# Softmax scaling of an attention kernel moved from ScalarE to GpSimd

## The chip, the cores and the metric

The kernel runs on one NeuronCore of a Trainium2 chip. Five engines work side by side, each through its own queue in order: TensorE (PE: matrix products and transposes, results in PSUM), VectorE (DVE), ScalarE (ACT), GpSimd (POOL) and SyncE (SP, which issues most transfers). They wait for each other by semaphores. SBUF is the on-chip memory of 128 partitions; PSUM is the accumulator memory, of which this kernel uses eight banks. The metric is the time of one execution on the device in microseconds (us); less is better.

## The reference

Two layers of an encoder on x of shape [1, 256, 1024] in float32. Each has a mixer of three kinds of attention side by side, and a gated feed-forward part:

```python
def mixer_sublayer(x, n1, w_in_l, ...):
    proj = rms_norm(x, n1) @ w_in_l                    # 1024 -> 2560
    qa, ka, va, qd, kd, vd, qc, kc, vc = jnp.split(proj, cuts, axis=-1)
    out_a = neighbourhood_attention(...)               # 4 heads of 64
    out_d = dilated_window_attention(...)              # 6 heads
    out_c = gqa_block_attention(...)                   # 6 heads on 2 of keys and values
    mix = jnp.concatenate([rms_norm(out_a, ...), rms_norm(out_d, ...), rms_norm(out_c, ...)], axis=-1)
    return x + mix @ w_out_l

def channel_sublayer(x, n2, w_gu, cw, cb, w_dn):
    g, u = jnp.split(rms_norm(x, n2) @ w_gu, 2, axis=-1)     # 1024 -> 2 x 2816
    g = depthwise_conv_centred(g, cw, cb)
    return x + (jax.nn.gelu(g, approximate=False) * u) @ w_dn
```

Every head is a softmax over 256 keys for each of 256 queries. The kernel computes all three kinds as one dense softmax, with masks and biases added to the scores where a kind has them:

```python
p = jax.nn.softmax(s, axis=-1)     # exp(s - max) / sum of it over the keys
```

## The kernel before

*Precision.* All large products are made of three products of split numbers: an operand z is split into hi (rounded by a copy on ScalarE) and lo = z - hi (VectorE), and hi x hi, hi x lo and lo x hi are added in PSUM (mm3, line 636). Weights come in units of up to 2048 columns: a transfer from HBM into a raw buffer (four of them), then hi by ScalarE and lo by VectorE in pieces of 512 columns (split, line 607), two units deep. The tiles are wp_raw, wp_hi and wp_lo. The subtraction for lo reads two tensors in SBUF, raw and hi. In layer 1, six units of the output projection have been split ahead and stored in HBM; their hi and lo are fetched by transfers that GpSimd issues (line 617).

*A layer.* The rows of x are scaled and transposed (split_T), projected in seven groups of columns, and the groups are normed and rotated head by head. Then come 16 heads, two at a time; the output projection; and the feed-forward part, which is two thirds of the time and in which TensorE runs without a gap.

*A head* (class Head, line 998). Its parts, with the engines that do them:

1. The scores of 256 queries (two tiles of 128 partitions, t = 0 and 1) by 256 keys: TensorE, into a bank of PSUM (scores, line 1151).
2. The largest score of each row: VectorE, with the bias added into a tile in SBUF where there is one.
3. The exponential with the row's sum as a second output (tile rs): ScalarE, into the tile p in SBUF, 128 x 256 for each t (lines 1016 and 1025).
4. The reciprocal of the sums, in place in rs: VectorE (line 1029).
5. Each row of p times its reciprocal, in place, one instruction for each t (lines 1030 and 1031): ScalarE. This is the step that changes. In the profile it is act_s2k<-act_s2k,small_rs.
6. Four transposes of 128 x 128 into a bank of PSUM: TensorE (turn, line 1033). In the profile they are psw_w<-const_ident,act_s2k.
7. The transposed p split into hi (act_ch, ScalarE) and lo (act_cl, VectorE).
8. The products with the values: TensorE (weigh, line 1049). Two heads share a result, which ScalarE and VectorE scale and split (mixed, line 1058); ScalarE squares it, and GpSimd adds up the squares of a group (act_sqm).

*What sets the order.* Nothing is issued as it is written. The kernel first records all operations (class Plan). Plan.order then plays them through: each has a cost in ns from the function cost (line 416), each pair of engines a time of handing over (HANDOVER, line 215), and of all operations that are ready the one that can start first is taken next, the earlier written one where two can. The outcome is the order of the five queues. So every recorded instruction shows line 413, the line that issues them, and groups are told apart by their tiles. Projections and output projections that wait for nothing fill TensorE's time between the parts of the heads. An operation of GpSimd without a rule of its own costs 2.2 ns an element and 160 ns; the costs of the plan decide on the order alone.

*GpSimd before.* It makes the reciprocal roots of the norms (small_ms, small_rstd), the tables of the rotations, the sums of squares, and the six pairs of transfers in layer 1.

*Buffers.* p, the biased scores, the squares and the feed-forward's tiles share five buffers (act_s2k). Scores, transposes, results of heads and feed-forward sums share four banks of PSUM (psw_w); the projections have the other four (psa_a).

Of the kernel before, what the change touches and what calls it, by code (L numbers as in the profile page):

```python
# [14 lines left out]
AF = mybir.ActivationFunctionType  # L15
ALU = mybir.AluOpType
# [3 lines left out]
S = 256  # L20
# [201 lines left out]
class Plan:  # L222
# [30 lines left out]
    def add(self, engine, method, args, kw):  # L253
# [14 lines left out]
        if method == "matmul" and not kw["start"]:  # L268
            ins.append(args[0])
        o.ns, o.size = cost(engine.name, method, args, kw, ins)  # L270
        o.before, o.after, o.first, o.tiles = set(), [], [], []
        for v in ins + outs:
# [143 lines left out]
def cost(engine, method, args, kw, ins):  # L416

    out = args[0]
    if method == "dma_start":
        w = out if isinstance(out, View) else args[1]  # L420
        small = min(out.shape[-1], args[1].shape[-1]) < 128
        return 460, 4 * math.prod(w.shape) * (2 if small else 1)
    n = out.width()
    psum = any(v.tile.pool.psum for v in ins)
    if engine == "PE":
        if method == "transpose":
            return 110, 0
        n = args[2].width()
        if args[1].dtype == F32:
            return 108, 0  # L430
        if args[1].shape[0] < P:
            return n / 4.8 + 15, 0
        return n / (2.4 if args[1].dtype == F32R else 1.2) + 2.5, 0
    if engine == "ACT":
        extra = 93 * sum(isinstance(kw.get(k), View) for k in ("scale", "bias")) + 90 * ("accum_out" in kw)
        return 0.833 * n + (47 if psum else 94) + extra, 0
    if engine == "DVE":
        if method in ("reduce_sum", "reduce_max"):
            n = args[1].width()
        per = 1.04  # L440
        if method in ("tensor_copy", "tensor_scalar_mul") and not psum:
            per = 0.52
        if method == "tensor_tensor_reduce":
            per = 1.3
        return per * n + (130 if method == "scalar_tensor_tensor" or method == "tensor_scalar_mul" and n > 16 else 70), 0
    if method == "memset":
        return 40 + 0.9 * n, 0
    if method == "tensor_copy":
        return 3.4 * n, 0
    if kw.get("op") == ALU.pow:  # L450
        return 300 + 165 * n, 0
    return 2.2 * n + 160, 0


@with_exitstack
def encoder_kernel(
# [21 lines left out]
    nc = Plan(tc)  # L478
# [337 lines left out]
    for l in range(DEPTH):  # L816
# [181 lines left out]
        class Head:  # L998
# [4 lines left out]
            def softens(self, sps):  # L1003

                name, bias = self.name, self.bias
                self.p = p = act.tile([P, NT, S], F32, tag="s2k", name=f"p_{name}", bufs=NS2K)
                nm = small.tile([P, NT], F32, tag="nm", name=f"nm_{name}")
                rs = small.tile([P, NT], F32, tag="rs", name=f"rs_{name}")

                if bias is not None:  # L1010
                    sb = act.tile([P, NT, S], F32, tag="s2k", name=f"sb_{name}", bufs=NS2K)
                    for t in range(NT):
                        nc.vector.tensor_tensor_reduce(
                            sb[:, t], sps[t], bias[t], -SCALE, 3e38, ALU.add, ALU.min, nm[:, t : t + 1]
                        )
                    for t in range(NT):
                        nc.scalar.activation(
                            p[:, t], sb[:, t], AF.Exp, bias=nm[:, t : t + 1], scale=-1.0,
                            accum_out=rs[:, t : t + 1],
                        )  # L1020
                else:

                    for t in range(NT):
                        nc.vector.reduce_max(nm[:, t : t + 1], sps[t], axis=AX.X, negate=True)
                    for t in range(NT):
                        nc.scalar.activation(
                            p[:, t], sps[t], AF.Exp, bias=nm[:, t : t + 1], accum_out=rs[:, t : t + 1]
                        )
                nc.vector.reciprocal(rs, rs)
                for t in range(NT):  # L1030
                    nc.scalar.activation(p[:, t], p[:, t], AF.Copy, scale=rs[:, t : t + 1])

            def turn(self):
                name = self.name
# [412 lines left out]
```

## Time and profile before

| | us |
|---|---|
| median of 3 runs | 616.48 (616.14 to 616.51) |
| the profiled execution | 616.62 |
| its span, from the first to the last instruction | 614.9 |
| TensorE busy | 605.8 (99%) |
| VectorE busy | 487.4 (79%) |
| ScalarE busy | 428.1 (70%) |
| GpSimd busy | 82.5 (13%) |

The profile is of one execution. Times within it are counted from the span's start. A row of a group gives the engine, the operation, the tile written, <-, the tiles read, partitions x elements, the count, then the busy time in us, the mean of one in ns, and the engine's idle time just before these instructions with what ended it. Rows in order of time give the start in us, the duration in us, the engine and the instruction, and in brackets the idle time before it; x4 stands for four in a row, merged, whose durations overlap a little, since an instruction starts while the one before drains. Rows of windows give the busy time of PE, PEld (loading of weights), DVE, ACT and POOL in a stretch with the number of instructions, then the granted clock of TensorE, the share of the transfer engines that was busy, and GB/s. Layer 0's heads lie between 44 and 116 us, those of layer 1 between 352 and 412 us, the two feed-forward parts behind them.

### The profile page before, as it was taken

What the parts mean: (1) busy time and instruction counts of PE and PEld (TensorE: products, weight loads), DVE (VectorE), ACT (ScalarE), POOL (GpSimd) and SP (SyncE); (2) the same over time, 40 slices, a digit from 0 to 9 for tenths busy, and PEclk for the clock granted to TensorE, in tenths of its full rate; (3) what the DMA queues carried; (4) which work ended last, traced back from release to release, by engine and by line L of the source; (5) the groups of instructions that cost most, each with busy time, mean ns of one, the idle gap of its engine ahead of it and who ended that gap; (6) DMA issues with size and microseconds to landing.
All of it is one profiled execution on the core that took longest, in us unless ns stands there. A gap on an engine that the chain in (4) does not pass through costs nothing.

```text
span 614.9 us, 9864 instructions
## 1 busy us (share of the span) xinstructions
PE 605.8 (99%) x3484; PEld 523.8 (85%) x3484; DVE 487.4 (79%) x1000; ACT 428.1 (70%) x1064; POOL 82.5 (13%) x136
## 2 busy tenths in 40 slices
PE   8999999999999999999999999999999999999997
PEld 6998878888888888888899988887888888888885
DVE  4898989897777988887867797867977777777774
ACT  6788989686566676666588898866755656556651
POOL 2731230211400000000022212332000000000000
PEclk9999999999999999999999999999999999999999
DMA  8794312655596999978444744553565556555501
GB/s 279 273 290 156 102 36 86 227 191 194 169 244 237 366 350 325 312 272 277 154 151 153 243 136 173 201 179 119 200 228 174 173 202 203 173 176 202 187 20 68
DMA packets 85073, 121.44 MB, mean 198 GB/s; under 512 B 9864, under 2 KB 69608, under 8 KB 85024
## 3 DMA queue, kind: packets, MB, share of 16 engines
q1 hardware_dynamic: 82752, 112.17, 55.3%
q0 software_dynamic: 1728, 8.39, 3.8%
q8 instruction: 27, 0.44, 0.3%
q10 hardware_dynamic: 544, 0.26, 0.2%
q14 instruction: 22, 0.18, 0.1%
HBM read 110.93 MB, written 9.88 MB: 196 GB/s over the span
## 4 chain that ended last, share of the span: by engine, by line
PE 93%; DVE 2%; ACT 2%; issue 1%; DMA 1%; POOL 0%; SPq 0%; DVEq 0%; ACTq 0%
PE psw_w L413 50%; PE psa_a L413 43%; DVE const_x L413 1%; ACT act_s2k L413 1%; DMA wp_raw<-in_w_in_dram 1%; DVE act_hT L413 1%; ACT act_hT L413 1%; ACT wp_hi L413 0%; DVE wp_lo L413 0%; POOL small_rstd L413 0%; ACT act_mixT_hi L413 0%; POOL small_ms L413 0%; SPq L413 0%; DVE act_mixT_lo L413 0%; DVE small_ss L413 0%
## 5 line engine op out<-in xcount | busy, mean ns | idle before, releaser
L413 DVE TENSOR_TENSOR wp_lo<-wp_raw,wp_hi 128x512 fp32r<-128x512 f32 (+2 forms) x332 | 232.9, 732 | 43.8 <-ACT wp_hi L413 42.3
L413 PE MATMUL psw_w<-act_hT,wp_hi 128*128 128x512 f32 x704 | 248.6, 397 | 0.4 <-DVE act_hT L413 0.4
L413 ACT CAST wp_hi<-wp_raw 128x512 fp32r<-128x512 f32 (+2 forms) x332 | 203.2, 661 | 27.0 <-PE psw_w L413 15.5
L413 PE MATMUL psw_w<-act_hT,wp_lo 128*128 128x256 f32 x704 | 196.5, 280 | 0.0
L413 PEld LDWEIGHTS psw_w<-act_hT,wp_hi 128*128 128x128 f32 x704 | 132.0, 188 | 32.6 <-DVE act_hT L413 1.1
L413 PEld LDWEIGHTS psw_w<-act_hT,wp_lo 128*128 128x128 f32 x704 | 132.7, 189 | 1.1
L413 PE MATMUL psa_a<-wp_hi,act_hT 128*128 128x384 f32 (+2 forms) x448 | 112.8, 332 | 0.7 <-ACT act_hT L413 0.5
L413 ACT COPY act_s2k<-psw_w 128x256 f32<-128x256 f32 x88 | 32.3, 372 | 74.5 <-PE psw_w L413 74.5
L413 PEld LDWEIGHTS psa_a<-wp_hi,act_hT 128*128 128x128 f32 x448 | 77.9, 189 | 3.8 <-ACT act_hT L413 1.0
L413 PE MATMUL psa_a<-wp_lo,act_hT 128*128 128x384 f32 (+2 forms) x224 | 74.8, 335 | 0.0
L413 PE MATMUL psa_a<-wp_lo,act_ch 128*128 128x512 f32 x176 | 69.5, 395 | 0.0
L413 PE MATMUL psa_a<-wp_hi,act_ch 128*128 128x512 f32 x176 | 69.4, 394 | 0.0
L413 PE MATMUL psa_a<-wp_hi,act_cl 128*128 128x512 f32 x176 | 65.8, 394 | 0.0
L413 DVE TENSOR_TENSOR act_s2k<-psw_w,act_s2k 128x256 f32<-128x256 f32 x88 | 36.8, 422 | 30.1 <-ACT act_s2k L413 29.7
L413 PEld LDWEIGHTS psa_a<-wp_lo,act_hT 128*128 128x128 f32 x224 | 42.3, 189 | 2.3 <-DVE wp_lo L413 1.3
L413 PEld LDWEIGHTS psa_a<-wp_hi,act_cl 128*128 128x128 f32 x176 | 33.2, 188 | 7.8
L413 PEld LDWEIGHTS psa_a<-wp_hi,act_ch 128*128 128x128 f32 x176 | 33.1, 188 | 7.8
L413 PEld LDWEIGHTS psa_a<-wp_lo,act_ch 128*128 128x128 f32 x176 | 33.1, 188 | 6.9
L413 DVE SCALAR_TENSOR_TENSOR act_s2k<-act_s2k,act_cw,act_s2k 128x255 f32<-128x255 f32 x88 | 36.9, 478 | 1.5 <-ACT act_s2k L413 1.3
L413 POOL TENSOR_TENSOR small_rstd<-small_ms,const_mh 128x6 f32<-128x6 f32 (+2 forms) x26 | 31.4, 1208 | 2.2
L413 ACT ACTIVATE act_s2k<-act_s2k,act_cw 128x256 f32<-128x256 f32 x44 | 24.1, 595 | 10.0 <-DVE act_s2k L413 9.6
L413 PE MATMUL psw_w<-act_ch,const_v 128*128 128x256 f32 x128 | 28.6, 286 | 1.1 <-ACT act_s2k L413 1.1
(112 smaller groups left out, 779.1 us busy)
## 6 DMA issues: line engine op xcount, KB each, us to landing
wp_raw<-in_w_gate_up_dram SPq DMA_DIRECT2D x44, 1024.0 KB, 5.1
wp_raw<-in_w_down_dram SPq DMA_DIRECT2D x22, 1024.0 KB, 4.8
wp_raw<-in_w_in_dram SPq DMA_DIRECT2D x14, 768.0 KB, 5.5
wp_raw<-in_w_in_dram SPq DMA_DIRECT2D x8, 1024.0 KB, 5.6
wp_raw<-in_w_out_dram SPq DMA_DIRECT2D x8, 768.0 KB, 6.3
dram_khi<-act_mixT_hi SPq DMA_DIRECT2D x4, 768.0 KB, 4.4
dram_klo<-act_mixT_lo SPq DMA_DIRECT2D x4, 768.0 KB, 5.8
wp_lo<-dram_klo POOLq DMA_DIRECT2D x4, 768.0 KB, 4.8
```

The lines of the kernel that those rows point to most:

```text
L413: getattr(o.engine.real, o.method)(*map(real, o.args), **{k: real(v) for k, v in o.kw.items()})
```

## The change

Step 5 is given to GpSimd, as a product with a scalar for each partition, still in place and still two instructions for a head: 32 heads in the two layers, so 64 instructions. The function cost gets a rule for it, 0.92 ns an element and 200 ns, which is 436 ns for 256 elements; n is the width of the output, and no other tensor_scalar has the width S = 256. The order of all queues is worked out anew from that.

```diff
@@ cost, the last lines: GpSimd @@
     if kw.get("op") == ALU.pow:
         return 300 + 165 * n, 0
+    if method == "tensor_scalar" and n == S:
+        return 0.92 * n + 200, 0
     return 2.2 * n + 160, 0
@@ Head.softens @@
                 nc.vector.reciprocal(rs, rs)
                 for t in range(NT):
-                    nc.scalar.activation(p[:, t], p[:, t], AF.Copy, scale=rs[:, t : t + 1])
+                    nc.gpsimd.tensor_scalar(p[:, t], p[:, t], rs[:, t : t + 1], None, ALU.mult)
```

## The prediction

> **What bounds the kernel now.** I read the page first, then the waits of the whole span, then the two attention stretches (44 to 116 us and 352 to 412 us) by windows, then single instructions in order of time.
>
> The page, span, busy times and the chain that ended last by engine:
>
> ```profile
> span 614.9 us, 9864 instructions
> ...
> PE 605.8 (99%) x3484; PEld 523.8 (85%) x3484; DVE 487.4 (79%) x1000; ACT 428.1 (70%) x1064; POOL 82.5 (13%) x136
> ...
> PE 93%; DVE 2%; ACT 2%; issue 1%; DMA 1%; POOL 0%; SPq 0%; DVEq 0%; ACTq 0%
> ```
>
> TensorE is busy or nearly so throughout, and 93% of the last chain is its own. A change on ScalarE can only be worth what TensorE waits. The waits say how much that is (engine, what waited, for whom, us, times, longest):
>
> ```profile
> PE psw_w L413 <- ACT act_s2k L413: 1.7, 2, 1.1
> PE psw_w L413 <- DVE const_x L413: 0.9, 2, 0.5
> ```
>
> The same view for 44 to 116 us alone has one more wait of TensorE:
>
> ```profile
> PE psw_w L413 <- DVE act_mixT_lo L413: 0.3, 1, 0.3
> ```
>
> So within the attention stretches TensorE stands still for 1.7 + 0.3 = 2.0 us, and, in the stretch from 412 to 426 us, 0.9 us more at the end of layer 1's mixer (the second row is the same there). That is all there is to win. The side engines are far fuller there than their averages over the span say (windows: PE, PEld, DVE, ACT, POOL busy):
>
> ```profile
> 44.00:116.00 72.00, 70.52 (x504) 61.63 (x503) 63.63 (x179) 63.55 (x195) 15.51 (x22) 1.00 0.34 111
> 352.00:412.00 60.00, 59.44 (x430) 51.92 (x430) 48.95 (x145) 50.83 (x150) 16.32 (x26) 1.00 0.46 162
> ```
>
> In layer 0 VectorE and ScalarE both work 88% of the stretch, with some 8.4 us of slack each, in layer 1 82% and 85%. GpSimd has over 40 us free in each. The granted clock is 1.00 in both.
>
> **The change part by part.** What is taken off ScalarE, by shape (count, busy us, mean ns):
>
> ```profile
> L413 ACT ACTIVATE act_s2k<-act_s2k,small_rs 128x256 f32<-128x256 f32 x64 | 28.1, 507 | 0.7 <-DVE small_rs L413 0.7
> ```
>
> 64 instructions go, all within the two stretches. In a row they overlap a little: four of them from 76.24 us take 1.71 us (below), so each occupies (1.71 - 0.51) / 3 = 0.40 us, and ScalarE gets back 64 x 0.40 = 26 us, 13 in each layer. Nearly all of it lies beside TensorE's work and is worth nothing. What is on the path is ScalarE's backlog ahead of TensorE's waits. The larger one, by time (start, duration, engine, what, idle before):
>
> ```profile
> 76.24 1.71 ACT L413 ACTIVATE act_s2k<-act_s2k,small_rs 128x256 f32<-128x256 f32 x4
> ...
> 80.70 0.47 ACT L413 ACTIVATE act_mixT_hi<-psw_w,const_gains 128x256 fp32r<-128x256 f32 x1 [0.30 <-PE psw_w L413]
> ...
> 82.04 0.47 ACT L413 ACTIVATE const_v<-psa_a,small_rx 128x256 fp32r<-128x256 f32 x1 [0.22 <-PE psa_a L413]
> ...
> 83.31 0.48 ACT L413 ACTIVATE act_s2k<-psw_w,small_nm 128x256 f32<-128x256 f32 x1
> ...
> 83.57 0.36 PE L413 MATMUL psw_w<-act_ch,const_v 128*128 128x256 f32 x1 [1.13 <-ACT act_s2k L413]
> ```
>
> 1.71 us of scales stand ahead of the exponentials that free the bank of PSUM for which TensorE waits 1.13 us. But ScalarE itself waited 0.30 and 0.22 us for TensorE in between, so a shorter backlog does not pass straight through. Of the 2.0 us I take half: -1.0. The ends are 0 and -2.0.
>
> What is put on GpSimd: 64 products of 128x256 by a column of scalars, two a head. No such operation is in the trace. The nearest rows:
>
> ```profile
> L413 POOL TENSOR_TENSOR act_sqm<-act_sqm,act_sqm 128x256 f32<-128x256 f32 x10 | 7.3, 734 | 32.0 <-ACT act_sqm L413 32.0
> L413 POOL COPY act_nab<-act_few 28x1984 f32<-28x1984 f32 x2 | 3.7, 1834 | 22.9 <-DMA act_few<-in_rpb_dram 22.9
> L413 POOL TENSOR_SCALAR small_ms<-small_ss,small_he 128x8 f32<-128x8 f32 x4 | 1.1, 275 | 12.7 <-DVE small_ss L413 12.5
> ```
>
> 275 ns (scalar from a column, 8 elements) is the lower end, 734 ns (256 elements, two tensors read) the upper. The copy with one input takes 1834 / 1984 = 0.92 ns an element. 275 + 248 x 0.92 = 503 ns, and I take 0.50 us: 16 us in each layer, within GpSimd's free 40. The Trainium skill's page "GPSIMD Engine Reference" (§ 3.1) gives 1.03 cycles an element at 1.2 GHz for bodies of up to two operations, an estimate of 0.22 us for 256 elements, and the copy's 0.92 ns agrees. By that figure on top of the 128x8 row it would be 0.49 us, and the sum would not move.
>
> Does the pair's latency matter? It does where the transposes follow a head's scales at once. Going through all 32 heads, in 15 (7 in layer 0, 8 in layer 1) the first transpose starts within 0.6 us after the second scale or before its end; in the other 17 it comes 0.9 to 5.1 us later. First and last of the 15:
>
> ```profile
> 50.55 0.16 DVE L413 RECIPROCAL small_rs<-small_rs 128x2 f32<-128x2 f32 x1
> 50.77 0.90 ACT L413 ACTIVATE act_s2k<-act_s2k,small_rs 128x256 f32<-128x256 f32 x2
> 52.12 0.27 PE L413 MATMUL psw_w<-const_ident,act_s2k 128*128 128x128 f32 x1
> ...
> 407.23 0.17 DVE L413 RECIPROCAL small_rs<-small_rs 128x2 f32<-128x2 f32 x1 [0.20 <-ACT act_s2k L413]
> 407.90 0.90 ACT L413 ACTIVATE act_s2k<-act_s2k,small_rs 128x256 f32<-128x256 f32 x2
> 408.65 0.60 PE L413 MATMUL psw_w<-const_ident,act_s2k 128*128 128x128 f32 x4
> ```
>
> ScalarE's pair takes 0.90 us, GpSimd's some 1.0: +0.10 for each of the 15. Against that, ScalarE began 0.06 us after the reciprocal in the first and 0.50 us after it in the last, since it had other work; GpSimd is mostly free, so about 0.25 us are saved. A hand-over from GpSimd to TensorE is not in the trace except at the start; I take it as equal to ScalarE's.
>
> Then there is a new cost, a block between GpSimd and VectorE, seen at two places in time order and in the small product's durations (min/median/max):
>
> ```profile
> 118.06 0.68 DVE L413 TENSOR_TENSOR wp_lo<-wp_raw,wp_hi 128x512 fp32r<-128x512 f32 x1
> 118.08 0.72 POOL L413 TENSOR_SCALAR small_ms<-small_ss 128x2 f32<-128x2 f32 x1 [1.38 <-DVE small_ss L413]
> ...
> 83.90 0.73 POOL L413 TENSOR_TENSOR act_sqm<-act_sqm,act_sqm 128x256 f32<-128x256 f32 x1
> 84.25 0.66 DVE L413 TENSOR_TENSOR act_z<-act_z,act_gna 128x256 f32<-128x256 f32 x1
> ```
>
> ```profile
> L413 POOL TENSOR_SCALAR small_ms<-small_ss x6: 191/192/719, 91.1 to 417.8; 128x2 f32<-128x2 f32 x6
> ```
>
> ```profile
> L413 DVE TENSOR_TENSOR act_z<-act_z,act_gna 128x256 f32<-128x256 f32 x2 | 0.8, 410 | 0.0
> ```
>
> A GpSimd product of 0.19 us takes 0.72 when it starts just behind a VectorE subtraction of two SBUF tensors, and ends 0.06 us after it: 0.53 us lost. The other way round, a VectorE product of two SBUF tensors takes 0.66 where it takes 0.41 in layer 1. The Trainium skill, "SBUF — State Buffer" (§ Who interferes with whom), states the rule behind it: a VectorE instruction with two SBUF inputs and a GpSimd instruction that reads SBUF exclude each other, and the second waits for the end of the first. The trace agrees: 118.08 + 0.72 = 118.80, against VectorE's end at 118.74. Taken to its end, this rule is the slower rival below.
>
> How often it will strike, from the subtractions that split the weights (VectorE, ScalarE busy in each stretch, only instructions on the raw weights):
>
> ```profile
> 48.00:116.00 68.00, 16.48 (x25) 13.49 (x25) 1.00 0.29 97
> 352.00:411.00 59.00, 7.14 (x11) 4.49 (x8) 1.00 0.46 162
> ```
>
> VectorE is in such an instruction 16.48 / 68 = 24% of layer 0's stretch and 12% of layer 1's. A GpSimd product that meets one waits half of 0.68 = 0.34 us on average; two a head make 2 x 0.34 x 0.24 = 0.16 us in layer 0, 0.08 in layer 1, mean 0.12. For a close head: 0.10 - 0.25 + 0.12 = -0.03 us, which is nothing. I enter 0, with ends of 15 x -0.15 = -2 and, if one of a head's two is always blocked, 15 x 0.34 = +5.
>
> VectorE pays too. GpSimd holds 16 us, 22% of layer 0's 72 and 27% of layer 1's 60; 25 x 0.22 = 5.5 and 11 x 0.27 = 3 subtractions wait half of 0.50 us: 1.4 + 0.7 = 2.1 us. VectorE's 8.4 us of slack in layer 0 cover most of that; what waits behind the delayed instruction are the split weights and the next head's maximum. I let a third through, +0.7, with ends 0 and +2.1.
>
> Last, the planner: it costs the new product and sets all five queues anew. Which order it finds cannot be read from this trace. It matters on GpSimd's queue in layer 1, where DMA issues stand that wait for TensorE:
>
> ```profile
> 371.50 0.79 POOL L413 DMA_DIRECT2D wp_lo<-dram_klo  x1 [5.34 <-PE psa_a L413]
> 372.28 0.55 POOL L413 DMA_DIRECT2D wp_hi<-dram_khi  x1
> ...
> 386.47 0.64 POOL L413 DMA_DIRECT2D wp_hi<-dram_khi  x1
> 387.11 0.54 POOL L413 DMA_DIRECT2D wp_lo<-dram_klo  x1
> ```
>
> A head's products behind such a pair come 387.11 + 0.54 - 386.47 = 1.18 us late at least; a rival again, 0 in the sum.
>
> The sum: -1.0 + 0 + 0.7 = -0.3 us on a span of 614.9. The profiled run took 616.62 us, 1.7 more than its span, so 616.3; the median of the runs is 0.14 lower, so **616.2 us**. I forecast no difference that can be told: a run of this kernel can be told from no change at about 0.2%, or 1.2 us.
>
> **The rivals.**
>
> *Faster.* All 2.0 us of waits in attention go with ScalarE's backlog, and the attention, done sooner, leaves TensorE more to do in the 0.9 us at the end of layer 1's mixer: 616.5 - 2.9 = 613.6 us. For it: ScalarE is the fuller of the two in layer 1 (50.8 against 49.0 us), and GpSimd picks up at once. Against: VectorE is as full in layer 0 and gains nothing.
>
> *Slower, the block.* If products and subtractions meet in most close heads, TensorE waits for the transposes' input: 15 x 0.34 = 5.1 us, less the 1.0 gained, 616.5 + 4.1 = 620.6 us. It decides from (1.0 + 1.2) / 0.34 = 6.5 of the 15 on. For it: a reciprocal on VectorE releases the products, and in the time order the next thing there is often a subtraction. Against: only a quarter of VectorE's time in layer 0 is of that kind.
>
> *Slower, GpSimd's queue.* If close heads of layer 1 come behind its 6 pairs of DMA issues: 8 of 16 heads are close, 6 x 0.5 x 1.18 = 3.5 us, so 616.2 + 3.5 = 619.7 us. Against it: a planner that knows when the buffer comes free can put the products first.
>
> **How the numbers follow.** No difference 0.38, around 616.2 (615.3 to 617.6); faster 0.29; the block 0.24; the queue 0.09. So faster by over 0.2% has 0.29, within it 0.38, slower 0.33. The range reaches below the faster rival's 613.6 for a shorter GpSimd latency, and just above the block's 620.6: 613.0 to 621.0.
>
> **What would show it.** Of the profile after: ScalarE's busy time down by about 28 us and GpSimd's up by 64 x 0.50 = 32; products of 0.50 us with a tail up to some 1.0 where a subtraction runs; TensorE's waits for ScalarE in attention down from 1.7 us to about half, with new waits for GpSimd on the transposes of p under 1 us in all; the subtractions of split weights in the stretches longer than the 0.68 us above. I am wrong if TensorE waits for GpSimd by several us, if the products take over 0.7 us alone, or if the time falls by over 1.2 us, which would mean that ScalarE's backlog held TensorE by more than the waits show.

## The result, and the profile after

The changed kernel takes 633.2 us (median of 4 runs, 632.3 to 633.4) against 616.3 us before: 1.0276 times as long (95% interval 1.0263 to 1.0288), some 17 us more. The forecast was 616.2 us within 613.0 to 621.0. Both the sign and the size were missed.

The page of the changed kernel, span, busy times and the last chain by engine:

```profile
span 631.4 us, 9950 instructions
...
PE 610.8 (97%) x3484; PEld 522.6 (83%) x3484; DVE 488.0 (77%) x1000; ACT 405.5 (64%) x1000; POOL 148.7 (24%) x200
...
PE 73%; POOL 9%; DVE 7%; issue 5%; ACT 3%; DMA 2%; SPq 0%; POOLq 0%; DVEq 0%; ACTq 0%
```

TensorE's own share of the last chain fell from 93% to 73%, and GpSimd, which had none, holds 9%. ScalarE was relieved of 22.6 us (428.1 to 405.5), against some 28 forecast; GpSimd took on 66 us (82.5 to 148.7), twice the 32 that the prediction allowed.

The products themselves and the waits of the whole span:

```profile
L413 POOL TENSOR_SCALAR act_s2k<-act_s2k,small_rs 128x256 f32<-128x256 f32 x64 | 64.8, 1026 | 32.3 <-DVE small_rs L413 32.2
```

```profile
L413 POOL TENSOR_SCALAR act_s2k<-act_s2k,small_rs x64: 909/922/1792, 50.4 to 418.9; 128x256 f32<-128x256 f32 x64
```

```profile
PEld psw_w L413 <- POOL act_s2k L413: 16.0, 27, 1.5
...
PE psw_w L413 <- POOL act_s2k L413: 8.0, 19, 1.2
...
PE psa_a L413 <- DMA wp_hi<-dram_khi: 2.3, 2, 1.6
```

The shortest product takes 0.91 us, the median 0.92, the mean 1.03. TensorE waits for GpSimd at 27 places (the loading of the transposes' operand, p, is the part that waits), 16.0 us in all by that queue and 8.0 us by the matrix engine behind it, which still drains earlier work in part of it. One head in order of time:

```profile
108.15 0.17 DVE L413 RECIPROCAL small_rs<-small_rs 128x2 f32<-128x2 f32 x1 [0.23 <-ACT act_s2k L413]
108.41 1.82 POOL L413 TENSOR_SCALAR act_s2k<-act_s2k,small_rs 128x256 f32<-128x256 f32 x2 [1.81 <-DVE small_rs L413]
109.38 0.14 PEld L413 LDWEIGHTS psw_w<-const_ident,act_s2k 128*128 128x128 f32 x1 [0.43 <-POOL act_s2k L413]
109.39 0.33 PE L413 MATMUL psw_w<-const_ident,act_s2k 128*128 128x128 f32 x1
110.28 0.31 PEld L413 LDWEIGHTS psw_w<-const_ident,act_s2k 128*128 128x128 f32 x3 [0.42 <-POOL act_s2k L413]
110.29 0.55 PE L413 MATMUL psw_w<-const_ident,act_s2k 128*128 128x128 f32 x3 [0.21 <-POOL act_s2k L413]
```

TensorE's queue reaches the first transpose before the first product is done, and the other three before the second is. The order was made for products of 0.44 us. TensorE takes its work in order, so whatever it could do meanwhile stands behind the transposes.

Where the time went, by TensorE's first long stretch of the last chain in each feed-forward part, before and then after (start, duration):

```profile
127.69 14.59 PE psw_w L413 x82
...
425.85 17.15 PE psw_w L413 x98
```

```profile
133.44 14.38 PE psw_w L413 x82
...
443.39 16.44 PE psw_w L413 x96
```

Layer 0's mixer ends 5.8 us later, layer 1's 17.5, so layer 1 lost about twice as much. The whole span is 16.5 us longer (614.9 to 631.4), so next to nothing was lost in the feed-forward parts.

### The profile page after: what moved, and what is told of

It reads as the page before. It is cut to its first block, busy times and chain, and to the rows that moved or that the text cites. A ratio compares the mean times of both kernels' runs of the same rounds, so it can differ in the third digit from the quotient of the medians.

```text
span 631.4 us, 9950 instructions
## 1 busy us (share of the span) xinstructions
PE 610.8 (97%) x3484; PEld 522.6 (83%) x3484; DVE 488.0 (77%) x1000; ACT 405.5 (64%) x1000; POOL 148.7 (24%) x200
## 4 chain that ended last, share of the span: by engine, by line
PE 73%; POOL 9%; DVE 7%; issue 5%; ACT 3%; DMA 2%; SPq 0%; POOLq 0%; DVEq 0%; ACTq 0%
PE psw_w L413 43%; PE psa_a L413 31%; POOL act_s2k L413 6%; ACT act_s2k L413 1%; POOL small_rstd L413 1%; DVE act_s2k L413 1%; DMA wp_hi<-dram_khi 1%; DVE const_x L413 1%; DVE small_nm L413 1%; DVE wp_lo L413 1%; DMA wp_raw<-in_w_in_dram 1%; ACT wp_hi L413 1%; POOL small_ms L413 1%; DVE act_cl L413 1%; DVE act_z L413 1%
## 5 line engine op out<-in xcount | busy, mean ns | idle before, releaser
L413 DVE TENSOR_TENSOR wp_lo<-wp_raw,wp_hi 128x512 fp32r<-128x512 f32 (+2 forms) x332 | 233.5, 733 | 42.8 <-ACT wp_hi L413 41.3
L413 PE MATMUL psa_a<-wp_hi,act_hT 128*128 128x384 f32 (+2 forms) x448 | 114.3, 334 | 0.9 <-ACT act_hT L413 0.7
L413 POOL TENSOR_SCALAR act_s2k<-act_s2k,small_rs 128x256 f32<-128x256 f32 x64 | 64.8, 1026 | 32.3 <-DVE small_rs L413 32.2
L413 POOL TENSOR_TENSOR small_s1x<-small_ssx 128x2 f32<-128x2 f32 x4 | 2.3, 576 | 180.0 <-ACT act_s2k L413 180.0
L413 ACT CAST act_ch<-psw_w 128x512 fp32r<-128x512 f32 x32 | 18.7, 585 | 26.2 <-PE psw_w L413 22.7
```

What stands on the lines that cost most here:

```text
L413: getattr(o.engine.real, o.method)(*map(real, o.args), **{k: real(v) for k, v in o.kw.items()})
```

## Experiments

Two theories at first. **P, the plan**: the queues were ordered for a product half as long as it is. **D, the duration**: a head's chain is longer and GpSimd fuller, whatever the order. And **B**, the block between GpSimd and VectorE, as a rival to both.

**The true cost.** The changed kernel with one number changed:

```diff
     if method == "tensor_scalar" and n == S:
-        return 0.92 * n + 200, 0
+        return 920, 0
```

> The changed kernel, but the planner is told what the product on GpSimd took in the changed kernel's profile, 920 ns instead of 436. Theory P (the plan): the 17 us come mostly from an order of the queues made for products half as long, so that TensorE meets transposes whose input is not there. Then the order made for 920 ns gives TensorE other work meanwhile, its waits for GpSimd fall from 8.0 us to under 2, and the time is 616 to 620 us. Theory D (the duration): a head's chain is longer by 1 us and two heads' products queue behind each other, whatever the order; the heads end later and TensorE runs out of other work. Then 626 to 633 us. Theory B (the block between GpSimd and VectorE): no change by the order, 630 to 634 us.

Measured: 619.5 us, 1.0063 times the kernel before (1.0048 to 1.0078). Each ratio here is to the kernel before as it ran beside that run (615.6 us here), so ratios are compared rather than times. Every engine does the same work as in the changed kernel, and some 13 of the 17 us are gone (1.0276 - 1.0063 = 2.1% of 616). The product is as slow as ever, but TensorE's waits for it:

```profile
L413 POOL TENSOR_SCALAR act_s2k<-act_s2k,small_rs x64: 911/926/1957, 50.3 to 411.6; 128x256 f32<-128x256 f32 x64
```

```profile
PEld psw_w L413 <- POOL act_s2k L413: 1.3, 5, 0.4
```

From 16.0 us at 27 places to 1.3 at 5. That is theory P by its own numbers; B falls as the main cause; D is left with 3.9 us.

**The same error without GpSimd.** The kernel before, in which only the planner is told another cost:

```diff
     if engine == "ACT":
+        if not psum and n == S and method == "activation" and args[2] == AF.Copy:
+            return 1, 0
```

> The kernel before, ScalarE scaling as ever; only the planner is told that each of these 64 instructions costs 1 ns where it assumed 400, so that a head's pair is planned 0.8 us too short. (In the changed kernel the pair is planned 0.97 us too short: 2 x (0.92 - 0.436).) No work of any engine differs from the kernel before, only the order. If an order made for too short a step is the cause of most of the 17 us, as 920 ns in the rule suggested (it took 13.7 us back), this slows too, by some 8 to 14 us: 624 to 630 us, with TensorE waiting for ScalarE's scales ahead of the transposes. If it is GpSimd itself that matters, 615 to 618 us.

Measured: 624.1 us, 1.0139 times (1.0121 to 1.0157), +8.5 us with no work changed. The waits are of the same kind, on ScalarE now:

```profile
PEld psw_w L413 <- ACT act_s2k L413: 8.0, 24, 0.7
```

So an order made for too short a step costs by itself.

**The error the other way.** The same place with 800 ns where 400 are true:

> The kernel before, with the planner told 800 ns for each scale on ScalarE where 400 are true: the error of the understated run (+8.5 us) the other way. If an order made for too long a step costs TensorE little, since its transposes come later than they could while other work fills in, 615 to 618 us. If any error of this size costs alike, 622 to 626 us.

Measured: 633.5 us, 1.0277 times (1.0248 to 1.0307). Neither of my expectations held: it is worse than the error in the other direction, and as bad as the change itself. TensorE does not wait for the scales; it runs out of prepared work elsewhere, at a few long places:

```profile
PE psw_w L413 <- DVE act_hT L413: 2.9, 3, 1.6
...
PE psw_w L413 <- ACT act_s2k L413: 2.3, 2, 1.2
...
PE psa_a L413 <- DMA wp_hi<-dram_khi: 2.2, 1, 2.2
PE psa_a L413 <- ACT act_mixT_hi L413: 1.9, 1, 1.9
```

The second row is transposes that wait although their scales are long done (at 386.07 us for the one at 390.23): an exponential that reads PSUM ends just before, at 390.09. And TensorE's granted clock falls after such places (windows: PE, PEld, DVE, ACT, POOL busy, clock):

```profile
380.00:400.00 20.00, 18.81 (x128) 16.37 (x128) 12.41 (x32) 14.04 (x42) 7.58 (x10) 0.91 0.39 139
400.00:420.00 20.00, 17.82 (x108) 14.29 (x108) 10.61 (x28) 10.59 (x32) 2.79 (x5) 0.91 0.42 152
420.00:440.00 20.00, 17.18 (x97) 13.92 (x94) 11.37 (x28) 10.91 (x30) 5.42 (x10) 0.91 0.34 107
```

Shorter windows show what the 0.91 is: the clock is at 0.50 for 3.4 us at a time, from 390, 414 and 424 us, and once more from 127 us, each time within 1.3 us of TensorE resuming after a wait (1.16, 2.18, 1.88 and 1.60 us). Four times 3.4 us at half the clock cost about 7 us, an estimate; the rest, some 11 us, comes with the order. The four runs agree: the one with a mean clock of 0.997 took 629.7 us, the two with 0.989 took 634.0 and 634.7.

**How much an order varies by itself.** The cost of the scales in the kernel before 10% off, and the product's cost in the changed kernel around the true one; each is one number in the rules shown.

> The kernel before, the planner told 360 ns for a scale on ScalarE instead of 400: an error of 10% that hardly makes a step late (0.08 us a head). If the time follows the size of the error, a tenth of what 399 ns too little did (+8.5 us): 616 to 617 us. If any new order brings its own few us, anything from 615 to 622.

> The same with 440 ns, 10% too much. By the size of the error a tenth of what 400 ns too much did (+17.7 us): 616 to 618 us. If any new order brings its own few us: 615 to 622.

> The changed kernel with 860 ns as the product's cost. 920 gave 619.5 us, 1050 gave 625.4. If GpSimd's load and the longer chain set what is left (3.9 us over the kernel before), 619 to 621 us here and with 980. If what is left is the luck of one order, the three costs scatter by several us on both sides of 619.5, down to 616.

> The same with 980 ns, between 920 (619.5 us) and 1050 (625.4). On a smooth curve 621 to 623 us; if each order has its own luck, anything from 616 to 626.

> The changed kernel with 1050 ns as the cost, the mean of a product in the run with 920 (the shortest 911 ns, and 8.8 us over that in all 64, from VectorE). If the rest of the loss there (619.5 us) is lateness that the plan does not know, 616 to 618 us; if it is GpSimd's load and the longer chain, 619 to 620 us.

Measured:

| cost told | time, us | ratio to the kernel before (95%) |
|---|---|---|
| ScalarE's scale, 1 ns | 624.1 | 1.0139 (1.0121 to 1.0157) |
| 360 | 616.3 | 1.0004 (0.9995 to 1.0013) |
| 440 | 618.3 | 1.0034 (1.0022 to 1.0046) |
| 800 | 633.5 | 1.0277 (1.0248 to 1.0307) |
| GpSimd's product, 436 (the change) | 633.2 | 1.0276 (1.0263 to 1.0288) |
| 860 | 621.8 | 1.0082 (1.0065 to 1.0099) |
| 920 | 619.5 | 1.0063 (1.0048 to 1.0078) |
| 980 | 621.3 | 1.0076 (1.0059 to 1.0093) |
| 1050 | 625.4 | 1.0150 (1.0136 to 1.0165) |

Around the true cost the time moves by 2 us or so from order to order. So the 3.9 us that GpSimd still costs with 920 ns are not one order's bad luck: 860, 920 and 980 all lie 4 to 5 us above the kernel before. Part of that is the clock. Told 920, the two runs with a mean clock of 1.000 took 618.5 and 619.1 us and the two with 0.997 took 620.0; in the profiled one TensorE waits 2.0 us for ScalarE's act_ch and then has 3.4 us at half the clock. At full clock the remainder is nearer 3 us. With 1050, the mean of a product including what holds it up, I expected 616 to 620 us; it got worse (625.4), and a mean clock of 0.995 to 0.997 explains only 2 to 3 us of that. So the remainder is not lateness that a longer cost cures.

**GpSimd's load without the path.** ScalarE scales as before; GpSimd makes 64 products nobody reads (planned at 920 ns), or writes zeros for as long:

```diff
                     nc.scalar.activation(p[:, t], p[:, t], AF.Copy, scale=rs[:, t : t + 1])
+                for t in range(NT):
+                    nc.gpsimd.tensor_scalar(spare[:, 1], spare[:, 0], rs[:, t : t + 1], None, ALU.mult)
```

> The kernel before, ScalarE scaling p as ever, and 64 products of the same form on GpSimd beside it: a spare tile of 128x256 times the head's reciprocals, whose result nobody reads. So GpSimd is as busy and meets VectorE as often as in the changed kernel, but nothing on the path waits for it except its own later work. Theory B: VectorE is blocked as often, the time is over 620 us. Theories P and D: 616 to 618 us.

```diff
-                nm = small.tile([P, NT], F32, tag="nm", name=f"nm_{name}")
+                nm = small.tile([P, 440], F32, tag="nm", name=f"nm_{name}")
...
                     nc.scalar.activation(p[:, t], p[:, t], AF.Copy, scale=rs[:, t : t + 1])
+                for _ in range(4):
+                    nc.gpsimd.memset(nm, 0.0)
```

> The kernel before with GpSimd kept busy beside it as in the run with 64 products aside (621.9 us, 1.0% over the kernel before), but by writes of zeros into the tile of the row maxima once a head is done with it, four of 0.46 us a head, that read nothing. Their sum, 1.86 us a head, is that of the two products. If products aside cost time because GpSimd and VectorE exclude each other when both read SBUF, this one is free: 615.5 to 617.5 us. If it is because GpSimd's own small work (the roots of the norms, the sums of squares, the fetches) queues behind them, it costs as much: 620 to 622.5 us. In between if both.

> The 64 products aside again (621.9 us), told to the planner as 1050 ns instead of 920, their mean there with the time they are held up by VectorE. The writes of zeros, which nothing holds up, cost 616.7 us. If the products aside are dear because they end later than planned, 617 to 619 us; if the exclusion itself costs, whatever the plan, 621 to 623 us.

Measured: the products aside 621.9 us, 1.0102 times (1.0085 to 1.0119); the zeros 616.7, 1.0031 (1.0019 to 1.0043); the products aside told as 1050 ns 625.3, 1.0155 (1.0140 to 1.0169). Spare products cost 6.3 us though nothing on the path reads them, and that is what theory B had expected (over 620 us), not P or D. Zeros of the same length cost 1.1 us by the medians and 1.9 by the ratio: six of the ten runs took 616.0 to 616.7 us, and four, with a mean clock of 0.996, 618.2 to 618.7. Durations on GpSimd, products aside and then zeros:

```profile
L413 POOL TENSOR_SCALAR const_spare<-const_spare,small_rs x64: 917/926/1949, 50.4 to 413.5; 128x256 f32<-128x256 f32 x64
```

```profile
L413 POOL MEMSET small_nm<- x128: 460/467/486, 49.6 to 408.2; 128x440 f32 x128
```

The products, which read SBUF, are stretched up to twice their length; the writes never. What GpSimd owes the path then comes late. First with products, then with zeros:

```profile
DVE act_z L413 <- POOL small_rstd L413: 8.9, 10, 2.0
```

```profile
DVE act_z L413 <- POOL small_rstd L413: 5.6, 9, 1.2
```

With products aside, VectorE waits 8.9 us for the roots of the norms, with zeros 5.6 (4.2 in the kernel before). TensorE, with products aside, waits more for the engines that feed it than the 1.7 us (ScalarE's act_s2k) and 0.4 us (VectorE's act_hT) of the kernel before:

```profile
PE psw_w L413 <- ACT act_s2k L413: 4.4, 4, 1.5
PE psw_w L413 <- DVE act_hT L413: 2.3, 3, 0.9
```

So GpSimd's reading load costs even off the path, and more (6.3 us) than the change does with the true cost; seven to eight tenths of that go with the reading. By which chain the products become these waits is not settled, and the two loads also differ in their order by up to the 2 us seen above. Telling the planner the products' mean made it 3.4 us worse, against both of my expectations; that is no more than its clock, since the runs told 920 ran at 1.000 and these at 0.993 to 0.997, which is 2 to 4 us.

**What a product costs.** Alone on GpSimd's queue in layer 0's feed-forward part:

> The kernel before with 33 products on spare tiles put on GpSimd's queue in layer 0's feed-forward part, where it has nothing to do: a tensor times a column of scalars and times a constant at 64, 128, 256 and 512 elements, a tensor times a tensor, a tensor times a broadcast column, and a copy, three of each, none in place. If the product with a column is slow in itself, 256 elements take 0.91 us as the shortest of three; if working in place made it slow, about 0.5. If the price is per element, 512 take about 1.6 to 1.8 us and 64 about 0.4; with the constant 0.1 us less if the column is a fixed price. The copy, by the row of 1984 elements, 0.24 to 0.4 us. The whole time stays at 616 us.

Single instructions, each the shortest of its three or within 0.01 us of it:

```profile
167.32 0.93 POOL L413 TENSOR_SCALAR const_spare<-const_spare,const_mh 128x256 f32<-128x256 f32 x1
179.24 0.37 POOL L413 TENSOR_SCALAR const_spare<-const_spare 128x64 f32<-128x64 f32 x1
181.79 0.53 POOL L413 TENSOR_SCALAR const_spare<-const_spare 128x128 f32<-128x128 f32 x1
184.88 0.92 POOL L413 TENSOR_SCALAR const_spare<-const_spare 128x256 f32<-128x256 f32 x1
189.69 1.49 POOL L413 TENSOR_SCALAR const_spare<-const_spare 128x512 f32<-128x512 f32 x1
191.27 0.74 POOL L413 TENSOR_TENSOR const_spare<-const_spare 128x256 f32<-128x256 f32 x1
195.41 0.94 POOL L413 TENSOR_TENSOR const_spare<-const_spare,const_mh 128x256 f32<-128x256 f32 x1
197.97 0.47 POOL L413 COPY const_spare<-const_spare 128x256 f32<-128x256 f32 x1
```

The product is slow in itself: 0.92 us for 256 elements in place or not, with a constant or a column. From 64 to 512 elements it is (1.49 - 0.37) / 448 = 2.5 ns an element. A product of two tensors is shorter than one with a scalar.

The last two rows are upper ends only: each of the three products with a broadcast column, and each of the three copies, started while VectorE was in an instruction with two inputs in SBUF. VectorE's next one was longer than usual in turn (two subtractions beside the products took 1.10 us each, where all 16 of that group took 0.68 to 0.69 in the kernel before).

The whole kernel took 619.1 us in its single run, 3.5 more than before, and not the 616 that I expected. The trace shows where: VectorE's subtractions for the split weights came late behind those it was held up in, TensorE waited 1.97 us for wp_lo at 199.92 us, and its clock was 0.60 and 0.55 in the two windows of 2 us behind that. So in this run the block seems to have reached TensorE, in a part where it was busy 199.99 of 200 us before (140 to 340 us).

**A shorter form.** The changed kernel with the product as a tensor_tensor, planned at 723 ns and then at the 610 ns it takes:

```diff
-                    nc.gpsimd.tensor_scalar(p[:, t], p[:, t], rs[:, t : t + 1], None, ALU.mult)
+                    nc.gpsimd.tensor_tensor(p[:, t], p[:, t], rs[:, t : t + 1].to_broadcast([P, S]), op=ALU.mult)
```

> The changed kernel with the product written as a tensor_tensor of p and the reciprocal broadcast along the row, which the planner costs at 2.2 ns an element and 160 ns, 723 ns. In the profile before, a tensor_tensor of this size on GpSimd took 734 ns. If it takes about that here, duration and cost agree. Theory P: 616 to 619 us. Theory D: between the two kernels, by (0.73 - 0.45) / (0.92 - 0.45) of the 17 us, about 626 us. Theory B: it reads two tensors, so as slow as the change or slower, 630 to 636 us.

> The product with the broadcast reciprocals again, which took 0.61 us in its profile where the planner assumed 0.72; now it is told 610 ns. A third less work on GpSimd than the tensor_scalar form. If the order's errors are all that is left, about 616 to 617.5 us; if GpSimd's load and the chain matter by their length, 617.5 to 619; no better than with 723 ns (619.4) if too long a cost does no harm.

Measured: 619.4 us, 1.0060 times (1.0039 to 1.0081), and with 610 ns 617.0 us, 1.0018 times (1.0009 to 1.0028). With the form a third shorter and the cost true, GpSimd does all the scales for 0.2% more than ScalarE did. The probe's 0.94 us for the same form is longer than this row of the last kernel; as said there, each of the three met an instruction of VectorE (the one shown began at 195.41 us, and a subtraction of VectorE ended at 195.88):

```profile
L413 POOL TENSOR_TENSOR act_s2k<-act_s2k,small_rs x64: 604/615/1167, 50.8 to 406.3; 128x256 f32<-128x256 f32 x64
```

**Half on each engine.** The first 128 queries on ScalarE, the others on GpSimd, in the 0.92 us form (planned at 920) and in the 0.61 us form (610):

```diff
-                for t in range(NT):
-                    nc.gpsimd.tensor_scalar(p[:, t], p[:, t], rs[:, t : t + 1], None, ALU.mult)
+                nc.scalar.activation(p[:, 0], p[:, 0], AF.Copy, scale=rs[:, 0:1])
+                nc.gpsimd.tensor_scalar(p[:, 1], p[:, 1], rs[:, 1:2], None, ALU.mult)
```

> One of a head's two products on ScalarE (the first 128 queries, 0.40 us), the other on GpSimd (0.92 us), with 920 ns as the planner's cost. They run side by side, so a head's chain is about as long as with ScalarE alone, GpSimd has half of the added load and ScalarE half of the relief. If what is left of the loss with the right cost (619.5 us) is the longer chain and GpSimd's load, half or more of it goes: 616 to 618 us; below 615 only if ScalarE's backlog is worth what the waits before showed (2.0 us).

> ScalarE scales the first 128 queries of a head, GpSimd the second 128 by the form with the broadcast reciprocals, which took 0.61 us, told to the planner as 610 ns. The split with the 0.92 us form gave 614.7 us. If GpSimd's length still costs there, 613.5 to 614.5; if TensorE has no more to give, the same within 0.2%.

Measured: 614.7 us, 0.9989 times the kernel before (0.9979 to 0.9998), and 613.9 us, 0.9973 times (0.9960 to 0.9985). The second beats both kernels by more than the forecast's 0.2%, if by little. Its attention stretches (PE, PEld, DVE, ACT, POOL busy):

```profile
44.00:116.00 72.00, 72.00 (x511) 62.80 (x510) 66.94 (x183) 58.64 (x174) 29.22 (x39) 1.00 0.36 117
352.00:412.00 60.00, 59.67 (x423) 51.29 (x422) 48.94 (x140) 43.27 (x128) 29.17 (x44) 1.00 0.50 170
```

TensorE was busy 70.52 of the first 72 us before and is busy 72.00 now, and 59.67 against 59.44 us in the second stretch; TensorE's own waits for act_s2k are gone. So 1.7 of the 2.0 us of waits that the prediction counted in attention were there to be won, with ScalarE relieved of half.

## Why the prediction was wrong

*The bound.* That TensorE bounds the kernel, and that only some 2 to 3 us were to be won, held as far as was tried: the best kernel here is 1.9 us faster than the kernel before run beside it (615.8).

*ScalarE's relief, entered as -1.0.* What the runs show fits it. TensorE's waits for ScalarE in layer 0's attention fell from 1.1 us to this one row (44 to 125 us of the changed kernel):

```profile
PE psw_w L413 <- ACT act_s2k L413: 0.2, 1, 0.2
```

In this kernel that alone proves little, since longer waits for GpSimd could hide them; the split kernels, which are faster, are the better evidence.

*The product's duration, the step that failed first.* "275 + 248 x 0.92 = 503 ns" put a copy's price an element on a product. Measured: 0.91 to 0.92 us alone, above even the 734 ns that I held for the upper end. The two-input row was no bound, since a product with a scalar is the slower of the two. The Trainium skill's figure in "GPSIMD Engine Reference" (§ 3.1), which I set beside the copy, is not borne out for this product either: 2.5 ns an element, three times what it gives. With that, the +0.10 us of a close head is +0.92: 1.82 us for a pair in the head shown, against 0.90. The prediction had named this as a sign of being wrong (over 0.7 us alone), and also waits of TensorE for GpSimd of several us; both came.

*The planner, entered as 0, the step that cost most.* I wrote that the order "cannot be read from this trace" and left its error out of the sum and out of the rivals. But the rule's cost of 436 ns stood in the change, and beside my own 503 it was already too short. An order made for a step planned 0.97 us a head too short was worth some 13 of the 17 us, and the kernel before shows the same with ScalarE alone (+8.5 us for 0.8 us a head). The two steps belong together: had a product taken 503 ns, the plan would have been 0.13 us a head short, and the run told 360 ns, 0.08 us a head short, lost nothing that can be told. So the mis-sized product is the root, and the planner the way by which most of it became time. A wrong cost was a rival in its own right: the price of being late for one close head, 0.5 to 1 us, times 15 and more heads.

*The block.* Its size was of the right order, its effect was not. The products' mean lies 1026 - 909 = 117 ns over the shortest, 0.23 us a head, against an estimate of 0.16 in layer 0 and 0.08 in layer 1. On VectorE's side the subtractions took 233.5 us in all against 232.9, so next to nothing of the 2.1 us allowed; with the true cost they took 234.9, which is 2.0 more. The rule of the Trainium skill ("SBUF — State Buffer", § Who interferes with whom) holds in the runs aside: products that read are stretched to as much as 1949 ns, writes of zeros stay within 486. As the rival that I priced, TensorE waiting in the close heads, it did not decide: with the true cost those waits are 1.3 us.

*GpSimd's queue.* The case that I priced at 3.5 us, products behind a transfer's issue, is in the changed kernel once: a head's reciprocals are done at 407.16 us, GpSimd stands until 408.21 at an issue that waits for TensorE, the products start at 408.89, and TensorE waits 0.7 us for them. The reverse cost more: TensorE waits 2.3 us for weights fetched by GpSimd, near the end of layer 1's mixer, where the kernel before has no such wait. The kernel before, told 1 ns for ScalarE's scale, has 1.1 us of it without any product on GpSimd, so it goes with the order at least in part. In the aside runs, the roots of the norms are what came late.

*What remains.* With the right cost, 4 to 5 us stay, of which 1 to 3 go with the lowered clock of most of those runs. A load of the same products off the path costs as much or more, and a form a third shorter leaves 1.1 us (0.18% of 616). That points to GpSimd's time in reading products, but it is not shown; by which waits exactly is open.

## What to carry to other kernels

Where an order is made from costs, a new cost is part of the change: measure the instruction alone on that engine in that form and size first, and price an error in it by the work that is tightly followed, in both directions. A row of another operation on the same engine is no bound, even if it does more. An engine with three quarters of its time free can still be too slow for a step on a tight chain, and splitting the step between the old engine and the new one may win where moving it loses.

## What the runs showed of the hardware

On GpSimd a product of a float32 tensor with a scalar costs 2.5 ns an element, more than a product of two tensors (0.92 against 0.74 us at 256 elements), and a copy at most half of it (0.47, beside instructions of VectorE that could hold it up). Written as a product with a broadcast column, in place, it took 0.61.

TensorE's granted clock fell to half for 3.4 us after waits of 1.2 to 2.2 us: 0.91 over each of three windows of 20 us in the run planned with 800 ns. Not after each: in the kernel before, a wait of 1.1 us left it at 1.00, and so did waits of 1.5 us with products aside and of 1.6 us in the changed kernel. So in these runs the length of the wait alone does not decide it. The Trainium skill's page "TensorE: Matmul & The Clock Gate" (Part 1) speaks of an idle window of some 3.4 us ahead of the lower clock; no wait in that run was that long, so here shorter ones were enough. So about 7 of that run's 17.7 us (the estimate above) are a slower clock after the waits, and not the waits themselves.
